# DeltaNet's values and two branches' gated outputs transposed by VectorE and a DRAM round trip

## The chip, the cores and the metric

One Trainium2 chip, one of its cores. The metric is device time in microseconds for one execution of the whole program; the profile is of one such execution. The engines are TensorE (PE, matmuls, with its weight loads as PEld), VectorE (DVE), ScalarE (ACT), GpSimd (POOL) and SyncE (SP); POOL and SP are also the queues from which most transfers are issued.

## The reference

One decoder layer on 256 positions of width 2048, in f32. The parts that bear on the change:

```
h = rms_norm(x, attn_norm)
(c_q, c_kv, k_rope, gla_q, gla_k, gla_v, gla_g_lr, gla_r,
 gdn_qkv, gdn_b, gdn_a, gdn_z, merge) = split(h @ w_in)
y_mla = mla_branch(...)                      # latent attention
y_gla = gla_branch(...)                      # gated linear attention, 4 heads of 128 x 256
y_gdn = gdn_branch(...)                      # gated DeltaNet, 8 value heads of 128
mixed = sum of sigmoid(merge_i) * (y_i @ w_branch_i)
x = x + mixed @ w_out
x = x + conv_ffn(rms_norm(x, ffn_norm))
out = rms_norm(x, final_norm)

# gdn_branch: q, k, v = split(silu(causal_dwconv(gdn_qkv))); chunked delta rule gives o
return rms_norm(o, out_norm).reshape(B, S, GDN_W) * silu(z)
# gla_branch: chunked scan gives o
return rms_norm(o, out_norm).reshape(B, S, GLA_W) * silu(r)
```

## The kernel before

**Weights and products.** The run is a sequence of products of an activation (256 positions) with weights of 1024 to 5632 rows. SP brings the weights in pieces `raw` of 512 KB (four buffers). ACT rounds a piece to `hi` (L191), DVE takes the rest `lo` (L103); both have four buffers, so a piece can be split only when PE is done with the piece four before it. PE forms each product from three matmuls (hi with hi, hi with lo, lo with hi). `f_chunk` (L196 to L198) gives 512 columns with features on the partitions: eight pieces of 24 matmuls, in two PSUM banks. `t_chunk` (L247 to L249) gives 512 columns with positions on the partitions: eight pieces of 12 wider matmuls, in two banks. Accumulators come from four banks `acc`; small products and transposes use four banks `mix` (`ps` in the rows).

**Order.** The program is written in one order and a tile scheduler sets each engine's order from it: it issues what is ready by its own model of times and waits, and the chip then runs each engine's list as it stands. SBUF tiles come from pools by tag, each tag with a number of buffers. A pool of one stage (`r2`: tags M, hq, g, Pm, vt, t, w) is closed and the next (`r3`: lqkv, glr, gates, E, aT, t) opened over the same memory; a tile of the next waits for the tiles that lay where it lies.

**DeltaNet.** Values come out of a convolution as `gv` (features on partitions). The solver needs them with positions on partitions: L780 transposes them on PE, four to a group of two heads, and DVE multiplies by `vs` out of PSUM into `vt`. Four groups are worked in two pairs. The results `og` (positions on partitions) are scaled by `z` and `fg` on DVE, and `gated_out` turns them back: four transposes on PE (L864) per group, then `gained` makes `hi_y` (ACT, L300) and `lo_y` (DVE, L106) out of PSUM. The region then changes to `r3`, and the GLA query, key and value chunks follow: `lq` and `lk` (tag lqkv) are emptied from `acc` by DVE, `lv` by ACT and DVE. `gated_out` serves GLA too, on `ol` with the gates `rs`, after the merge of branch 2 and ahead of the merge of branch 1; its results are `hi_E` and `lo_E`.

**Turning by DVE.** The kernel already has another way: `turned` (L303) transposes blocks of 32 by 32 on DVE into `tr`, POOL writes `tr` to DRAM (`d_t`, L313), and POOL reads it back with the blocks in their places (`rd`, L319, four transfers to a group); `gained_sb` (L323) then does what `gained` does, out of SBUF. It is used for the merge's first three column blocks and for the first three of the second half's input.

Of the kernel before, what the change touches and what calls it, by code (L numbers as in the profile page):

```python
# [9 lines left out]
F32 = mybir.dt.float32  # L10
# [6 lines left out]
P = 128  # L17
# [38 lines left out]
def trunk(ctx, tc, A, out, dbg=None, stop=None):  # L56
    nc = tc.nc
    pe, dve, act, pool, sync = nc.tensor, nc.vector, nc.scalar, nc.gpsimd, nc.sync
    serial = [0]

    def nm(s):
        serial[0] += 1
        return f"{s}{serial[0]}"
# [3 lines left out]
    dp = ctx.enter_context(tc.tile_pool(name="scratch", bufs=1, space=bass.MemoryType.DRAM))  # L67
# [14 lines left out]
    def S(tag, shape=(P, 512), dt=F32, n=None):  # L82
        p, bufs = pools[tag]
        return p.tile(list(shape), dt, name=nm(n or tag), tag=tag, bufs=bufs)

    def PS(n="ps"):
        return pp.tile([P, 512], F32, name=nm(n), tag="mix")
# [7 lines left out]
    def keep(shape, n, dt=F32):  # L95
        return cp.tile(list(shape), dt, name=n)
# [5 lines left out]
    def tt(o, a, b, op, eng=None):  # L102
        (eng or dve).tensor_tensor(o, a, b, op=op)  # L103
# [4 lines left out]
    MUL, ADD, SUB = ALU.mult, ALU.add, ALU.subtract  # L108
# [184 lines left out]
    def gained(psb, gains, store):  # L293

        hi, lo = store.new()
        if not isinstance(store, Joint):
            hi, lo = ([v[:, j] for j in range(2)] for v in (hi, lo))
        for j, g in enumerate(gains):
            src = psb[:, j * 256:(j + 1) * 256]
            act.activation(hi[j], src, AF.Copy, scale=g)  # L300
            stt(lo[j], src, g, hi[j], MUL, SUB)

    def turned(src, tags, n=512):  # L303

        nk = n // P
        d = dp.tile([2 * P, n], F32, name=nm("d_t"))
        for t in range(2):
            v = S(tags[0], (P, n), n="tr")  # L310
            dve.transpose(v.rearrange("p (b k i) -> p k b i", b=4, k=nk),
                          src[t].rearrange("p (k b i) -> p k b i", b=4, k=nk))
            pool.dma_start(d[t * P:(t + 1) * P], v)  # L313
        dv = d.rearrange("(a j) (b k i) -> b j a k i", j=32, b=4, k=nk)
        res = []
        for g in range(nk // 2):
            r = S(tags[1], (P, 8, 2, 32), n="rd")
            for b in range(4):
                pool.dma_start(r[b * 32:(b + 1) * 32], dv[b, :, :, 2 * g:2 * g + 2])  # L319
            res.append(r)  # L320
        return res

    def gained_sb(r, gains, store):  # L323

        hi, lo = store.new()
        if not isinstance(store, Joint):
            hi, lo = ([v[:, j] for j in range(2)] for v in (hi, lo))
        for j, g in enumerate(gains):
            h_, l_ = (v[j].rearrange("p (a i) -> p a i", i=32) for v in (hi, lo))
            act.activation(h_, r[:, :, j], AF.Copy, scale=g)  # L330
            stt(l_, r[:, :, j], g, h_, MUL, SUB)
# [302 lines left out]
        stt(gdec[:, t, :], xg[:, t, :], -1.0, ea, MUL, MUL)  # L634


    sel = keep([P, 68], "sel", F32R)
    pool.memset(sel.bitcast(F32), 0.0)
    pool.memset(sel[:, 3:4].bitcast(F32), 1.0)
# [133 lines left out]
    for gp in ((0, 1), (2, 3)):  # L773

        vts = {}
        for g in gp:
            psb = PS().rearrange("p (t x) -> p t x", t=2)
            for a in range(2):
                for t in range(2):
                    pe.transpose(psb[:, t, a * P:(a + 1) * P], gvv[2 * g + a][:, t * P:(t + 1) * P], ident)  # L780
            vts[g] = S("vt", (P, 2, 2, P))
            tt(vts[g].rearrange("p t a d -> p t (a d)"), psb, vs[:, :, g:g + 1].to_broadcast([P, 2, 256]), MUL)
        for s in (32, 64):
            work = []
            Pms = {g: S("Pm", (P, 4, s), n="Pm") for g in gp}
            for p in range(64 // s):
                for g in gp:
                    b1, b2 = slice(2 * p * s, 2 * p * s + s), slice(2 * p * s + s, 2 * p * s + 2 * s)
                    psb = PS()
                    pv = [psb[:, k * 128:k * 128 + 4 * s].rearrange("p (u j) -> p u j", u=4) for k in  # L790
                          ((0, 1, 2) if s == 32 else (0, 2))]
                    work.append((b1, b2, pv, Pms[g], Ms[g], Ys[g], Xs[g]))
            for b1, b2, pv, Pm, M, Y, X in work:
                for u in range(4):
                    pe.matmul(pv[0][b2, u, :], M[b1, u, b2], X[b1, u, b1], start=True, stop=True, **sk)
                dve.tensor_copy(Pm[b2], pv[0][b2])
            for b1, b2, pv, Pm, M, Y, X in work:
                for u in range(4):
                    pe.matmul(pv[1][b1, u, :], Pm[b2, u, :], Y[b2, u, b2], start=True, stop=True, **sk)
                dve.tensor_scalar(Y[b1, :, b2], pv[1][b1], -1.0, None, op0=MUL)  # L800
            if s == 32:
                for b1, b2, pv, Pm, M, Y, X in work:
                    for u in range(4):
                        pe.matmul(pv[2][b2, u, :], Y[b2, u, b2], Pm[b2, u, :], start=True, stop=True, **sk)
                    dve.tensor_scalar(X[b2, :, b1], pv[2][b2], -1.0, None, op0=MUL)
        u0s, W0s, R1s, W1s = {}, {}, {}, {}
        for g in gp:
            u0s[g] = PS()
            for a in range(2):
                pe.matmul(u0s[g][:, a * P:(a + 1) * P], Ys[g][:, a * 2, :], vts[g][:, 0, a, :], start=True, stop=True)  # L810
            W0s[g] = S("w", (P, 2, P), n="W0")
            tt(W0s[g], u0s[g][:, :256].rearrange("p (a d) -> p a d", a=2), b3(wj[:, 0, 2 * g:2 * g + 2], P), MUL)
        for g in gp:
            for a in range(2):
                pe.matmul(u0s[g][:, 256 + a * P:256 + (a + 1) * P], hqs[g][1][:, 1, a, :], W0s[g][:, a, :],
                          start=True, stop=True)
            R1s[g] = S("w", (P, 2, P), n="R1")
            tt(R1s[g], vts[g][:, 1], u0s[g][:, 256:].rearrange("p (a d) -> p a d", a=2), SUB)
        for g in gp:
            u1 = PS()  # L820
            for a in range(2):
                pe.matmul(u1[:, a * P:(a + 1) * P], Ys[g][:, a * 2 + 1, :], R1s[g][:, a, :], start=True, stop=True)
            W1s[g] = S("w", (P, 2, P), n="W1")
            tt(W1s[g], u1[:, :256].rearrange("p (a d) -> p a d", a=2), b3(wj[:, 1, 2 * g:2 * g + 2], P), MUL)
        for g in gp:
            op = PS().rearrange("p (t a d) -> p t a d", t=2, a=2)
            q0, q1 = hqs[g]
            for a in range(2):
                pe.matmul(op[:, 0, a, :], q0[:, 0, a, :], W0s[g][:, a, :], start=True, stop=True)
                pe.matmul(op[:, 1, a, :], q0[:, 1, a, :], W0s[g][:, a, :], start=True, stop=False)  # L830
                pe.matmul(op[:, 1, a, :], q1[:, 0, a, :], W1s[g][:, a, :], start=False, stop=True)
            os_ = S("d", (P, 2, 2, P), n="og")
            dve.tensor_copy(os_, op)
            o_gdn.append(os_)
            for a in range(2):
                for t in range(2):
                    junk = S("t", (P, P), n="junk")
                    c = t * 8 + 2 * g + a
                    act.activation(junk, os_[:, t, a, :], AF.Square, accum_out=gst[:, c:c + 1])
# [12 lines left out]
    for t in range(2):  # L852
        dve.tensor_scalar(fg[:, t, :], fg[:, t, :], rx[:, t:t + 1], None, op0=MUL)

    def gated_out(o_tiles, f_of, zs, gcol, name, ytag):

        y = Act(8, ytag)
        for g in range(4):
            o = o_tiles[g]
            f_of(g, o, [zs[t][g // 2][:, (g % 2) * 256:(g % 2) * 256 + 256] for t in range(2)])  # L860
            psb = PS()
            for a in range(2):
                for t in range(2):
                    pe.transpose(psb[:, a * 256 + t * P:a * 256 + (t + 1) * P], o[:, t, a, :], ident)  # L864
            gained(psb, [half_gain[:, gcol + 2 * g + a:gcol + 2 * g + a + 1] for a in range(2)], y)
            if dbg is not None and ("y_" + name) in dbg:
                full = S("t", (P, 2, 256), n="dbg")
                tt(full, y.hi[g].bitcast(F32), y.lo[g], ADD)
                sync.dma_start(dbg["y_" + name][:, 2 * g:2 * g + 2, :], full)
        return y  # L870
# [51 lines left out]
            tt(ov, ov, z[t], MUL)  # L922
        tt(o, o, fg[:, :, 2 * g:2 * g + 2].unsqueeze(3).to_broadcast([P, 2, 2, P]), MUL)

    y_gdn = gated_out(o_gdn, scale_gdn, zs, 8, "gdn", "y")
    if stop == "gdn":
        return

# [137 lines left out]
            ov = o[:, t].rearrange("p a d -> p (a d)")  # L1066
            stt(ov, ov, fl8[:, 2 * g + t:2 * g + t + 1], z[t], MUL, MUL)

    y_gla = gated_out(o_gla, scale_gla, sr, 0, "gla", "E")
    if stop == "gla":  # L1070
        return

# [206 lines left out]
```

## Time and profile before

| | |
|---|---|
| median of 3 runs | 1680.28 us (1678.97 to 1680.73) |
| profiled execution | 1680.61 us, span 1678.8 us |
| PE busy | 1664.4 us, 99% of the span |
| PE weight loads | 1426.9 us, 85% |
| DVE busy | 1099.7 us, 66% |
| ACT busy | 820.1 us, 49% |
| POOL busy | 123.9 us, 7% |
| moved by DMA | 315.01 MB, mean 188 GB/s |

The page gives busy times over the whole span and the chain of work that ended last; groups of instructions have the line, the engine, the operation and the tiles (output, then inputs, buffer numbers left out), and the idle time ahead of them with what ended it. Transfers are shown with their time from issue to landing. Many rows carry the line of a helper, such as L103 for each two-operand operation of DVE, so tiles tell more than lines.

### The profile page before, as it was taken

Reading aid. Unit: us, or ns where it says so; the run is one execution under the profiler, and the core shown is the slowest. Engines: PE = TensorE matmul, PEld = TensorE weight load, DVE = VectorE, ACT = ScalarE, POOL = GpSimd, SP = SyncE. Lnnn points to the kernel's source line nnn. Section 1 sums busy time; section 2 is a strip of 40 time slices with the busy share of each in tenths; the row PEclk is TensorE's granted clock in tenths of the full one; section 3 lists DMA queues with packets and bytes.
Section 4 is the critical chain, followed back from the end, with each engine's and each line's share of the span. In section 5 each row is a group of like instructions: output and inputs, shape, how many; then the busy total and the mean of one; then the engine's idle time right before and its main releaser. Section 6 shows DMA issues by size and latency. Waiting matters only on the chain.

```text
span 1678.8 us, 24640 instructions
## 1 busy us (share of the span) xinstructions
PE 1664.4 (99%) x9468; PEld 1426.9 (85%) x9468; DVE 1099.7 (66%) x1721; ACT 820.1 (49%) x1132; POOL 123.9 (7%) x193
## 2 busy tenths in 40 slices
PE   9999999999999999999999999999999999999997
PEld 7999988878998888888888888888888888888886
DVE  6956788855745696665556766664566665456666
ACT  6554563433434655444545555554355553345454
POOL 1000013110000000002112100000000000000000
PEclk9999999999999999999999999999999999999999
DMA  7654456654466565558777665555665566665663
GB/s 255 166 187 130 145 170 181 203 161 152 146 187 198 163 197 157 181 189 255 240 220 243 216 190 187 188 187 191 193 194 188 189 189 195 193 190 189 194 186 119
DMA packets 168774, 315.01 MB, mean 188 GB/s; under 512 B 17786, under 2 KB 20530, under 8 KB 168656
## 3 DMA queue, kind: packets, MB, share of 16 engines
q1 hardware_dynamic: 163200, 301.83, 57.1%
q0 software_dynamic: 5424, 11.60, 2.4%
q8 instruction: 74, 1.21, 0.3%
q14 instruction: 44, 0.36, 0.1%
q10 hardware_dynamic: 32, 0.01, 0.0%
HBM read 307.63 MB, written 5.77 MB: 187 GB/s over the span
## 4 chain that ended last, share of the span: by engine, by line
PE 98%; DMA 1%; SPq 0%; ACT 0%; DVE 0%; issue 0%; ACTq 0%
PE acc L249 17%; PE acc L248 17%; PE acc L247 17%; PE acc L228 10%; PE mix L228 10%; PE acc L229 5%; PE mix L229 5%; PE acc L198 3%; PE acc L196 3%; PE acc L197 3%; DMA x<-in_x_dram 1%; PE ps L542 0%; PE acc L1203 0%; PE acc L1205 0%; PE acc L1204 0%; PE ps L541 0%
## 5 line engine op out<-in xcount | busy, mean ns | idle before, releaser
L103 DVE TENSOR_TENSOR lo<-raw,hi 128x1024 fp32r<-128x1024 f32 (+2 forms) x571 | 686.1, 1203 | 511.3 <-ACT hi L191 508.0
L191 ACT CAST hi<-raw 128x1024 fp32r<-128x1024 f32 (+2 forms) x555 | 582.3, 1049 | 725.1 <-PE acc L249 414.9
L248 PE MATMUL acc<-lo,hi_h 128*128 128x512 f32 x640 | 249.5, 392 | 0.0
L247 PE MATMUL acc<-hi,hi_h 128*128 128x512 f32 x640 | 247.3, 391 | 1.6 <-ACT hi_h L300 1.2
L249 PE MATMUL acc<-hi,lo_h 128*128 128x512 f32 x640 | 248.9, 391 | 0.0
L228 PE MATMUL acc<-hl_h,hi 128*128 128x512 f32 x704 | 246.3, 396 | 0.0
L228 PE MATMUL mix<-hl_h,hi 128*128 128x512 f32 x704 | 246.3, 395 | 0.0
L229 PE MATMUL mix<-hl_h,lo 128*128 128x256 f32 x704 | 196.0, 278 | 0.0
L229 PE MATMUL acc<-hl_h,lo 128*128 128x256 f32 x704 | 195.7, 279 | 0.0
L228 PEld LDWEIGHTS mix<-hl_h,hi 128*128 128x128 f32 x704 | 132.1, 188 | 31.5
L228 PEld LDWEIGHTS acc<-hl_h,hi 128*128 128x128 f32 x704 | 131.8, 188 | 30.9
L247 PEld LDWEIGHTS acc<-hi,hi_h 128*128 128x128 f32 x640 | 119.9, 188 | 27.6 <-ACT hi_h L300 1.6
L248 PEld LDWEIGHTS acc<-lo,hi_h 128*128 128x128 f32 x640 | 120.2, 188 | 24.9 <-DVE lo L103 0.5
L249 PEld LDWEIGHTS acc<-hi,lo_h 128*128 128x128 f32 x640 | 120.0, 188 | 24.3
L229 PEld LDWEIGHTS acc<-hl_h,lo 128*128 128x128 f32 x704 | 132.5, 188 | 0.6
L229 PEld LDWEIGHTS mix<-hl_h,lo 128*128 128x128 f32 x704 | 132.5, 188 | 0.0
L248 PE MATMUL acc<-lo,hi_f 128*128 128x512 f32 x320 | 124.3, 389 | 0.0
L247 PE MATMUL acc<-hi,hi_f 128*128 128x512 f32 x320 | 124.2, 389 | 0.0
L249 PE MATMUL acc<-hi,lo_f 128*128 128x512 f32 x320 | 124.0, 389 | 0.0
L198 PE MATMUL acc<-hi_h,lo 128*128 128x256 f32 (+1 forms) x400 | 114.1, 285 | 0.0
L196 PE MATMUL acc<-hi_h,hi 128*128 128x256 f32 (+1 forms) x400 | 114.1, 285 | 0.0
L197 PE MATMUL acc<-lo_h,hi 128*128 128x256 f32 (+1 forms) x400 | 113.9, 285 | 0.0
(399 smaller groups left out, 2265.9 us busy)
## 6 DMA issues: line engine op xcount, KB each, us to landing
raw<-in_w_in_dram SPq DMA_DIRECT2D x207, 512.0 KB, 3.4
raw<-in_ffn_w_up_dram SPq DMA_DIRECT2D x176, 512.0 KB, 4.3
raw<-in_ffn_w_down_dram SPq DMA_DIRECT2D x88, 512.0 KB, 4.7
raw<-in_w_out_dram SPq DMA_DIRECT2D x32, 512.0 KB, 4.7
raw<-in_w_branch_mla_dram SPq DMA_DIRECT2D x16, 512.0 KB, 3.8
raw<-in_w_branch_gdn_dram SPq DMA_DIRECT2D x16, 512.0 KB, 3.6
raw<-in_w_branch_gla_dram SPq DMA_DIRECT2D x16, 512.0 KB, 6.1
raw<-in_mla_w_ukv_dram SPq DMA_DIRECT2D x8, 512.0 KB, 4.0
```

The costliest lines, as they stand in the source:

```text
L103: (eng or dve).tensor_tensor(o, a, b, op=op)
L191: act.copy(hi[:, ks], raw[:, ks])
L196: pe.matmul(o, s_hi, m_hi, start=first, stop=False, skip_group_check=True)
L197: pe.matmul(o, s_hi, m_lo, start=False, stop=False, skip_group_check=True)
L198: pe.matmul(o, s_lo, m_hi, start=False, stop=last, skip_group_check=True)
L228: pe.matmul(banks[f], hi[:, kt, fs], joint[k], start=k == 0, stop=False, skip_group_check=True)
L229: pe.matmul(banks[f][:, :T], lo[:, kt, fs], joint[k][:, :T], start=False, stop=k == nk - 1, skip_group_check=True)
L247: pe.matmul(o, ah, hi[:, kt, :], start=first, stop=False)
L248: pe.matmul(o, ah, lo[:, kt, :], start=False, stop=False)
L249: pe.matmul(o, al, hi[:, kt, :], start=False, stop=last)
```

## The change

Three places that transposed on PE go the other way.

- Values: after L634 DVE turns each `gv` group in blocks of 32 into a `tr` tile (tag t) and POOL writes it to DRAM (`d_v`). Where L780 stood, POOL reads a group back in four transfers into `rd` (tag t), and DVE multiplies by `vs` in two instructions per group.
- `gated_out` of DeltaNet: `turned` with 256 columns (two transposes, two writes and four reads for a group) with the tags t and g, then `gained_sb`.
- `gated_out` of GLA: the same, both tags lqkv.

So 48 transposes leave PE (16 for values, 16 for each output). DVE gets 4 transposes of 128x512 and 16 of 128x256; POOL's queue gets 20 writes and 48 reads. The other lines of the kernel are as they were; the scheduler orders everything anew.

```diff
+    d_v = []
+    for g in range(4):
+        v = S("t", (P, 4, 4, 32), n="tr")
+        dve.transpose(v.rearrange("p b k i -> p k b i"), gv[g].rearrange("p a (t b i) -> p (a t) b i", t=2, b=4))
+        d = dp.tile([P, 4, 4, 32], F32, name=nm("d_v"))
+        pool.dma_start(d, v)
+        d_v.append(d.rearrange("(a j) b k i -> b j a k i", j=32))
...
         for g in gp:
-            psb = PS().rearrange("p (t x) -> p t x", t=2)
-            for a in range(2):
-                for t in range(2):
-                    pe.transpose(psb[:, t, a * P:(a + 1) * P], gvv[2 * g + a][:, t * P:(t + 1) * P], ident)
+            r = S("t", (P, 4, 2, 2, 32), n="rd")
+            for b in range(4):
+                pool.dma_start(r[b * 32:(b + 1) * 32].rearrange("p c a t i -> p c (a t) i"), d_v[g][b])
             vts[g] = S("vt", (P, 2, 2, P))
-            tt(vts[g].rearrange("p t a d -> p t (a d)"), psb, vs[:, :, g:g + 1].to_broadcast([P, 2, 256]), MUL)
+            for t in range(2):
+                dve.tensor_scalar(vts[g][:, t].rearrange("p a (c i) -> p a c i", i=32),
+                                  r[:, :, :, t].rearrange("p c a i -> p a c i"), vs[:, t, g:g + 1], None, op0=MUL)
...
-    def gated_out(o_tiles, f_of, zs, gcol, name, ytag):
+    def gated_out(o_tiles, f_of, zs, gcol, name, ytag, tags):
...
-            psb = PS()
-            for a in range(2):
-                for t in range(2):
-                    pe.transpose(psb[:, a * 256 + t * P:a * 256 + (t + 1) * P], o[:, t, a, :], ident)
-            gained(psb, [half_gain[:, gcol + 2 * g + a:gcol + 2 * g + a + 1] for a in range(2)], y)
+            r, = turned([o[:, t].rearrange("p a d -> p (a d)") for t in range(2)], tags, 256)
+            gained_sb(r, [half_gain[:, gcol + 2 * g + a:gcol + 2 * g + a + 1] for a in range(2)], y)
...
-    y_gdn = gated_out(o_gdn, scale_gdn, zs, 8, "gdn", "y")
+    y_gdn = gated_out(o_gdn, scale_gdn, zs, 8, "gdn", "y", ("t", "g"))
...
-    y_gla = gated_out(o_gla, scale_gla, sr, 0, "gla", "E")
+    y_gla = gated_out(o_gla, scale_gla, sr, 0, "gla", "E", ("lqkv", "lqkv"))
```

The order on the engines at the end of the DeltaNet branch. First place, DVE, before: `og_3339` is the last scaled output, `lo_4942` to `lo_5002` are weight pieces of the GLA key chunk, `lq` is the query chunk's result out of `acc`.

```order
L103 TENSOR_TENSOR og_3339<-og_3339,fg 128x512
L103 TENSOR_TENSOR lo_4942<-raw_4939,hi_4941 128x1024
L103 TENSOR_TENSOR lo_4972<-raw_4969,hi_4971 128x1024
L106 SCALAR_TENSOR_TENSOR lo_y_4608<-ps_4602,half_gain,hi_y_4607 128x256
L106 SCALAR_TENSOR_TENSOR lq_4659<-acc_4663,rbc 128x512
L106 SCALAR_TENSOR_TENSOR lo_y_4622<-ps_4616,half_gain,hi_y_4621 128x256
L106 SCALAR_TENSOR_TENSOR lo_y_4636<-ps_4630,half_gain,hi_y_4635 128x256
L106 SCALAR_TENSOR_TENSOR lo_y_4650<-ps_4644,half_gain,hi_y_4649 128x256
L106 SCALAR_TENSOR_TENSOR lo_y_4608<-ps_4602,half_gain,hi_y_4607 128x256
L106 SCALAR_TENSOR_TENSOR lq_4660<-acc_4664,rbc 128x512
```

DVE there in the changed kernel: `lo_5170` is the last piece of the key chunk, `lo_5204` to `lo_5258` are the first four of the value chunk, `tr_4689` is the last of the eight transposes.

```order
L103 TENSOR_TENSOR lo_5170<-raw_5167,hi_5169 128x1024
L311 STREAM_TRANSPOSE tr_4689<-og_3359 128x2x4x32
L103 TENSOR_TENSOR lo_5204<-raw_5201,hi_5203 128x1024
L103 TENSOR_TENSOR lo_5222<-raw_5219,hi_5221 128x1024
L106 SCALAR_TENSOR_TENSOR lo_y_4635<-rd_4629,half_gain,hi_y_4634 128x256 x2
L103 TENSOR_TENSOR lo_5240<-raw_5237,hi_5239 128x1024
L103 TENSOR_TENSOR lo_5258<-raw_5255,hi_5257 128x1024
L106 SCALAR_TENSOR_TENSOR lo_y_4656<-rd_4650,half_gain,hi_y_4655 128x256 x2
L106 SCALAR_TENSOR_TENSOR lo_y_4677<-rd_4671,half_gain,hi_y_4676 128x256 x2
L106 SCALAR_TENSOR_TENSOR lo_y_4698<-rd_4692,half_gain,hi_y_4697 128x256 x2
L106 SCALAR_TENSOR_TENSOR lq_4707<-acc_4711,rbc 128x512
L106 SCALAR_TENSOR_TENSOR lq_4708<-acc_4712,rbc 128x512
```

The first `lq` stood behind the first `lo_y` and two pieces of the key chunk; it now stands behind all `lo_y` and four pieces of the value chunk.

Second place, PE, before: a group's transposes (`ps_4644`) inside the query chunk, whose banks are `acc_4663` and `acc_4664`, and the start of the key chunk (`acc_4907`).

```order
L197 MATMUL acc_4664<-lo_h_220,hi_4877 128x256
L864 MATMUL ps_4644<-ident,og_3339 128x128 x4
L198 MATMUL acc_4664<-hi_h_219,lo_4878 128x256
L196 MATMUL acc_4664<-hi_h_219,hi_4877 128x256
L197 MATMUL acc_4664<-lo_h_220,hi_4877 128x256
```

PE in the changed kernel at the end of the key chunk (`acc_4956`) and the start of the value chunk, whose bank `acc_5199` is the one that `acc_4711` had.

```order
L198 MATMUL acc_4956<-hi_h_219,lo_5170 128x256
L196 MATMUL acc_4956<-hi_h_219,hi_5169 128x256
L197 MATMUL acc_4956<-lo_h_220,hi_5169 128x256
L198 MATMUL acc_4956<-hi_h_219,lo_5170 128x256
L247 MATMUL acc_5199<-hi_5203,hi_h_142 128x512
L248 MATMUL acc_5199<-lo_5204,hi_h_142 128x512
```

The transposes are gone, and the value chunk follows the key chunk directly in both kernels; the bank that it opens with is now emptied by the `lq` of the first place.

Third place, POOL's queue from the solver's results to the GLA inputs, before:

```order
L764 MEMSET Y_3001 128x512
L767 DMA Y_3001<-d_y 32x4x32 x4
L764 MEMSET Y_3009 128x512
L767 DMA Y_3009<-d_y 32x4x32 x4
L951 DMA glr_5767<-in_onerow_dram 1x16x16
```

and in the changed kernel:

```order
L788 DMA rd_3209<-d_v_2668 32x4x128 x4
L313 DMA d_t_4622<-tr_4623 128x256
L313 DMA d_t_4622<-tr_4626 128x256
L313 DMA d_t_4643<-tr_4644 128x256
L313 DMA d_t_4643<-tr_4647 128x256
L313 DMA d_t_4664<-tr_4665 128x256
L319 DMA rd_4629<-d_t_4622 32x8x64 x4
L313 DMA d_t_4664<-tr_4668 128x256
L313 DMA d_t_4685<-tr_4686 128x256
L319 DMA rd_4650<-d_t_4643 32x8x64 x4
L313 DMA d_t_4685<-tr_4689 128x256
L319 DMA rd_4671<-d_t_4664 32x8x64 x4
```

Between the solver and the GLA inputs the queue now has the values' reads and the eight writes and sixteen reads of the four groups; the last four reads (`rd_4692`) follow the rows shown.

## The prediction

> **What bounds the kernel now.** I read the busy times of the page first, then the chain that ended last, then TensorE's (PE) busy time by stretches of the span, then what PE waited for.
>
> ```profile
> PE 1664.4 (99%) x9468; PEld 1426.9 (85%) x9468; DVE 1099.7 (66%) x1721; ACT 820.1 (49%) x1132; POOL 123.9 (7%) x193
> ...
> PE 98%; DMA 1%; SPq 0%; ACT 0%; DVE 0%; issue 0%; ACTq 0%
> ```
>
> ```profile
> 17.00:270.00 253.00, 253.00 (x1698) 229.25 (x1697) 195.49 (x400) 138.84 (x237) 17.84 (x21) 1.00 0.55 167
> 270.00:460.00 190.00, 190.00 (x1202) 162.01 (x1202) 131.20 (x232) 75.77 (x109) 20.37 (x40) 1.00 0.56 169
> 460.00:720.00 260.00, 260.00 (x1651) 218.36 (x1650) 171.31 (x331) 130.66 (x163) 6.00 (x19) 1.00 0.58 180
> 720.00:1640.00 920.00, 920.00 (x4711) 783.36 (x4711) 568.63 (x683) 448.12 (x567) 73.21 (x96) 1.00 0.63 201
> ```
>
> ```profile
> PE acc L247 <- ACT hi_h L300: 1.2, 1, 1.2
> PE acc L1203 <- ACT hi_f L276: 1.1, 1, 1.1
> PE warm L159 <- DVE ones L155: 1.1, 1, 1.1
> PE ps L371 <- DMA x<-in_x_dram: 0.6, 2, 0.4
> PE acc L247 <- ACT hi L191: 0.5, 1, 0.5
> ```
>
> In the second fence stand, for each stretch, its length and the busy time of PE, of its weight loads, DVE, ACT and POOL, then the granted clock and the share of the DMA engines. From 17 to 1640 us PE is busy without a gap, and all its waits of the run come to 4.5 us, at the two ends. So whatever work is taken off PE between 17 and 1640 us shortens the run by its length, and every microsecond in which PE is made to wait there lengthens it by one. The other engines matter only where they stop PE. Every place that the change touches lies between 230 and 730 us.
>
> **What is taken off PE.** 48 transposes: 16 at L780 (values), 16 at L864 on `og` and 16 at L864 on `ol`.
>
> ```profile
> L780 PE MATMUL ps<-ident,gv x16: 272/272/273, 273.4 to 397.3; 128*128 128x128 f32 x16
> ...
> L864 PE MATMUL ps<-ident,og x16: 270/272/276, 453.9 to 456.1; 128*128 128x128 f32 x16
> ...
> L864 PE MATMUL ps<-ident,ol x16: 270/272/273, 706.2 to 715.6; 128*128 128x128 f32 x16
> ```
>
> ```profile
> 454.01 0.44 PE ps L864 x4
> ...
> 714.46 1.42 PE ps L864 x13
> ```
>
> The 272 ns of one are latency; what counts is the pitch. In the chain, four take 0.44 us and thirteen 1.42, 0.11 each. 48 x 0.11 = 5.3 us, all inside the gapless part: **-5.3 us**.
>
> **What is added, and where it hides.** DVE gets 4 transposes of 128x512 and 16 of 128x256.
>
> ```profile
> L311 DVE STREAM_TRANSPOSE tr<-x x6: 669/686/704, 869.9 to 914.0; 128x512 f32<-128x512 f32 x6
> ...
> L106 DVE SCALAR_TENSOR_TENSOR lo_d<-rd,hi_d x12: 416/418/426, 768.4 to 838.8; 128x256 fp32r<-128x256 f32 x12
> ```
>
> That is 4 x 0.69 + 16 x 0.34 (half the size, half the time: an estimate) = 8.2 us; the four products out of PSUM become eight of half the size out of SBUF, and a `lo_y` goes from 0.48 us to the 0.42 of `lo_d`. DVE has 57 us free in the first stretch, 59 in the second and 89 in the third, so its total costs nothing; the order on DVE is what counts. POOL gets 20 writes and 48 reads:
>
> ```profile
> L319 POOL DMA_DIRECT2D rd<-d_t x48: 582/584/613, 760.3 to 924.9; - x48
> ...
> DMA to landing us min/median/max: 3.4/5.2/6.7
> ```
>
> ```profile
> L313 POOL DMA_DIRECT2D d_t<-tr x12: 547/553/580, 752.6 to 915.0; - x12
> ...
> DMA to landing us min/median/max: 2.4/3.7/6.0
> ```
>
> 20 x 0.55 + 48 x 0.58 = 39 us of issue on a queue that is 7% busy. The traffic is 3 MB written and 3 MB read beside 315 MB, with the DMA engines at 0.56 to 0.58: no price by itself. SP's queue, which brings the weights, is passed by none of it.
>
> **Where PE will wait: the end of the DeltaNet branch.** This is the term that decides. In the profile, DVE and ACT do this there:
>
> ```profile
> 450.33 2.50 DVE L103 TENSOR_TENSOR og<-og,fg 128x512 f32<-128x512 f32 x4
> 452.75 2.41 DVE L103 TENSOR_TENSOR lo<-raw,hi 128x1024 fp32r<-128x1024 f32 x2
> 455.08 0.48 DVE L106 SCALAR_TENSOR_TENSOR lo_y<-ps,half_gain,hi_y 128x256 fp32r<-128x256 f32 x1
> 455.47 0.68 DVE L106 SCALAR_TENSOR_TENSOR lq<-acc,rbc 128x512 f32<-128x512 f32 x1
> ```
>
> ```profile
> 447.09 1.05 ACT L191 CAST hi<-raw 128x1024 fp32r<-128x1024 f32 x1 [1.83 <-PE acc L197]
> 449.97 1.05 ACT L191 CAST hi<-raw 128x1024 fp32r<-128x1024 f32 x1 [1.83 <-PE acc L197]
> ```
>
> `lq` empties the PSUM bank of the GLA query chunk within a fraction of a microsecond of the first `lo_y`, while PE is already in the key chunk. In the changed order (first place shown above) `lq` and `lk` stand behind all eight `lo_y` on DVE, because their SBUF tiles lie where the branch's `tr` and `rd` tiles lie, and those are read until the last `lo_y`. There are four accumulator banks: two hold the query chunk, two the key chunk, and the first matmul of the value chunk (second place) needs the first one back. So PE ends the key chunk and has nothing else in its order until `lq` is through. Behind the waiting `lo_y` on DVE stand the splits of the value chunk's weights and both `lk`.
>
> How long? Call E the end of the key chunk. A weight piece takes PE 2.88 us here (449.97 - 447.09) and four pieces are held.
> - By DVE: `lo_5258`, four rows ahead of `lq`, belongs to the piece that takes the slot of the key chunk's last piece, so its cast can begin only at E: 1.05 us of cast, 1.2 of `lo`, six `lo_y` of 0.42 and an `lq` of 0.68 make 5.5 us, with a tenth or two for the releases 5.7.
> - By POOL (third place): the last `tr` comes behind `lo_5170`, whose slot is free at E - 11.5, so at about E - 8.9. In the built program each transfer of this queue also waits for the one eight places ahead of it. With 0.58 us an issue, 3.7 us for a write and 5.2 for a read, the second group's reads go out from E - 9.3, the last write at E - 6.5, the third group's from E - 5.9, the last read of the fourth at E - 1.3, held up by the third before it. It lands at E + 3.9; cast, two `lo_y`, `lq` and the releases make it 6.0 to 6.5.
>
> The later of the two holds: **+6.3 us**. The ends: with reads of 3.4 us DVE's way governs and it is 5.7; with reads of 6.7 the extra 1.5 us counts in each of three rounds, and it is about 10. I take the median, since the DMA share here (0.56) is below that of the stretch in which it was measured (0.63).
>
> On this wait the Trainium skill, page "DMA: Bandwidth & Descriptors", section "Anatomy of one DMA — SWDGE (gpsimd) path", gives about 2.0 us fixed and bytes over 436 GB/s, so 2.15 us for a 64 KB read. By that POOL's way would be over before DVE's, and the sum below would be lower by 0.6. The row says 5.2 us for these reads, and the row is used.
>
> **What the wait does to PE's clock.** PE has not been idle this long anywhere before its end.
>
> ```profile
> 1660.00:1670.00 10.00, 8.95 (x54) 7.79 (x52) 8.03 (x26) 5.34 (x16) 0.00 (x0) 1.00 0.30 102
> 1670.00:1673.50 3.50, 0.00 (x0) 0.00 (x0) 2.87 (x13) 1.26 (x3) 0.00 (x0) 1.00 0.03 11
> 1673.50:1674.00 0.50, 0.00 (x0) 0.00 (x0) 0.00 (x0) 0.08 (x1) 0.00 (x0) 0.93 0.80 311
> 1674.00:1674.50 0.50, 0.00 (x0) 0.00 (x0) 0.00 (x0) 0.00 (x0) 0.00 (x0) 0.50 1.09 418
> ```
>
> ```profile
> 437.19 0.22 PE ps L829 x2
> ```
>
> ```profile
> 1.06 3.78 PE L159 MATMUL warm<-ones 128*128 128x128 f32 x16 [1.06 <-DVE ones L155]
> ```
>
> PE's last matmul ends near 1669; the granted clock falls to 0.50 at about 1673.9, some 5 us later. And the sixteen first matmuls of the run, after idleness, took 0.24 us each where a pair of the same shape later takes 0.22: they ran at half speed for 3.8 us (the clock column reads 1.00 there, the durations say otherwise). So 3.8 us at half speed lose 1.9 us. A wait of 6.3 us is longer than the 5 at the end: **+1.9 us**, between 0 (no drop) and 2.5.
>
> The Trainium skill, page "TensorE: Matmul & The Clock Gate", section "Part 1: The HAM clock gate (the "warmup" mystery)", has the clock halved after an idle window of about 3.4 us that runs free of the kernel. By it a 6.3 us wait need not hold a whole window: in one run of seven it would not (0.5 of 3.4), and the sum would be 1.9 lower; the trace, with one drop after 5 us, does not contradict it.
>
> **The other places.** Values: `rd` for groups 2 and 3 lies in the `t` tag and can only be issued late; DVE may stand at the product for up to 1.7 us (the read's 5.2 less the 3.4 at best), but between there and the solver's products PE has chunk matmuls in its order. GLA: the round trip runs beside the gate chunk of the merge, 96 matmuls of 0.23 us, 22 us; four groups at the pace above take about 18 to 20 from the first `tr`, so it is covered with 2 to 4 us left. The front: the squares before L648 share the `t` tag with the four written values and wait for those writes; PE's reads of them now stand about 95 rows further down, behind chunk matmuls, and I leave 1 to 2 us of margin. These three: 0, with 0 to 3 in the range.
>
> **Sum**, against the profiled execution (1680.61 us; its span is 1678.8, with 1.8 around it): -5.3 + 6.3 + 1.9 = +2.9. The median of the runs is 1680.28, 0.33 below; from it 1683.2 us.
>
> **Rivals.**
> - Wait, but no drop of the clock: -5.3 + 5.7 to 6.3 = +0.4 to +1.0, 1681.0 us. For it: the only drop seen came after 5 us, so 5.7 is close. Against it: the start shows that idleness halves the speed.
> - The wait does not come, and the time falls by the 5.3 us: 1675.0 us, the other side. The place is the `lq` row; it decides in this way if DVE reaches `lq` before E, which needs `lo_5258` not to hang on the key chunk's last piece. For it: such round trips are hidden elsewhere (the merge's `turned` cost PE no wait in the list above). Against it: the order on DVE puts it behind a piece that can't be cast before E, whatever the transfers do.
> - More than one wait: on top of the forecast the front's writes take 6.0 us instead of 3.7 (2.3 more) and the values' reads stop the solver's products by 1.7: +6.9, 1687.2 us. For it: the margins are of the size of the spread of the landings. Against: chunk matmuls stand in between.
>
> **How the numbers follow.** About 0.2%, 3.4 us, is what a measurement of this kernel can tell from no change: 1676.9 to 1683.6. The forecast (wait and clock, 1682.6 with a wait of 5.7 us to 1685.6 with reads of 6.0) has 0.60; no drop of the clock 0.17; more than one wait 0.15; no wait 0.08. The forecast's case straddles the bound: half of it, 0.30, lies above, with the third rival 0.45 slower; 0.30 + 0.17 = 0.47 the same; 0.08 faster. The range leaves out the case without a wait and the upper third of the case with several: 1680.0 to 1688.0.
>
> **What would show it.** No L780 or L864 on PE. One gap of 5.7 to 7 us on PE at the first L247 of the value chunk, near 480 us, released by DVE's `lq`; a granted clock of 0.50 behind it for about 4 us; ahead of `lq` on DVE six `lo_y` without a stop, or with one that DMA `rd` ended (POOL's way). POOL busy by about 39 us more. I am wrong if that gap is under 5 us, if there is a second gap of over a microsecond at L648, L805 or the first matmul on `hi_E`, or if the clock holds through the gap.

## The result and the profile after

| | before | changed |
|---|---|---|
| median of 5 runs | 1680.28 us (1678.86 to 1680.73) | 1689.76 us (1688.76 to 1690.35) |
| ratio | | 1.0057 (95%: 1.0046 to 1.0068) |
| profiled execution, span | 1680.61, 1678.8 us | 1688.76, 1687.0 us |

The change makes the kernel 9.5 us slower; 2.9 were forecast, with a range up to 1688.0. The profiled execution is the quickest of the five, so the traces explain 8.2 us of span.

The page of the changed kernel, busy times and chain:

```profile
PE 1665.5 (99%) x9420; PEld 1425.0 (84%) x9420; DVE 1108.1 (66%) x1745; ACT 819.8 (49%) x1132; POOL 162.3 (10%) x261
...
PE 95%; issue 3%; DMA 1%; POOL 1%; ACT 0%; DVE 0%; SPq 0%; ACTq 0%; POOLq 0%
```

What PE waited for, in the changed kernel (the two longest):

```profile
PE acc L247 <- DVE lq L106: 8.0, 1, 8.0
PE acc L1210 <- ACT hi_f L276: 1.1, 1, 1.1
```

PE has 48 transposes less to do and is yet busy 1.1 us longer. Of waits one is new: the first matmul of the GLA value chunk for DVE's `lq`, 8.0 us, at the place that was named. The chain of the changed kernel around it (start, length, what):

```profile
472.61 4.49 DMA d_t<-tr
...
477.67 1.33 POOL rd L319 x3
...
479.39 4.38 DMA rd<-d_t
...
483.87 0.52 ACT hi_y L330
...
484.41 0.44 DVE lo_y L106
...
485.21 0.69 DVE lq L106
485.91 0.14 issue
486.05 0.77 PE acc L247
```

PE's last key matmul ends at 478.07. The last write of the round trip goes out at 472.61 and takes 4.5 us, the fourth group's reads wait for it, take 1.7 to issue and 4.4 to land, then cast, `lo_y` and `lq` follow: POOL's way, not DVE's, ends last. POOL's own row for these reads:

```profile
477.67 2.30 POOL L319 DMA_DIRECT2D rd<-d_t  x4 [2.08 <-DMA d_t<-tr]
```

Behind the wait the granted clock is down (stretches of 1 us of the changed kernel; the columns as in the prediction):

```profile
488.00:489.00 1.00, 1.00 (x4) 0.81 (x3) 0.00 (x0) 0.00 (x0) 0.00 (x0) 0.50 0.00 0
489.00:490.00 1.00, 1.00 (x4) 0.77 (x4) 0.00 (x0) 0.00 (x0) 0.00 (x0) 0.69 0.00 0
```

A clock of 0.69 over 489 to 490 means half speed up to 489.62; from 486.05 that is 3.6 us at half speed, 1.8 lost. So far: -4.1 (what the transposes proved to be worth in the traces, below) + 8.0 + 1.8 = +5.7. The other 2.5 us of the 8.2 are in no wait and not in the clock. They had to be found.

### The profile page after: what moved, and what is told of

Its sections match the earlier page's. It is cut to its first block, busy times and chain, and to the rows that moved or that the text cites. A ratio compares the mean times of both kernels' runs of the same rounds, so it can differ in the third digit from the quotient of the medians.

```text
span 1687.0 us, 24708 instructions
## 1 busy us (share of the span) xinstructions
PE 1665.5 (99%) x9420; PEld 1425.0 (84%) x9420; DVE 1108.1 (66%) x1745; ACT 819.8 (49%) x1132; POOL 162.3 (10%) x261
## 4 chain that ended last, share of the span: by engine, by line
PE 95%; issue 3%; DMA 1%; POOL 1%; ACT 0%; DVE 0%; SPq 0%; ACTq 0%; POOLq 0%
PE acc L248 17%; PE acc L247 17%; PE acc L249 17%; PE acc L228 10%; PE mix L228 10%; PE acc L229 5%; PE mix L229 5%; PE acc L198 3%; PE acc L196 3%; PE acc L197 3%; DMA rd<-d_t 1%; PE ps L542 0%; PE acc L1210 0%; PE acc L1212 0%; PE acc L1211 0%
```

## The experiments

All runs are compared with the kernel before, whose median was 1680.0 to 1680.2 beside each of them. Differences between two variants are differences of their medians, unless a trace is named.

**DeltaNet's output alone.** Values and GLA's output put back on PE:

```diff
-    y_gla = gated_out(o_gla, scale_gla, sr, 0, "gla", "E", ("lqkv", "lqkv"))
+    y_gla = gated_out(o_gla, scale_gla, sr, 0, "gla", "E", None)
```

(With `None`, `gated_out` transposes on PE; the lines for the values are those of the kernel before. The rest of the edit is left out here.)

> Only DeltaNet's gated output goes by DVE and DRAM; values and GLA's output stay on PE as before. Theory A (one wait: the first lq stands behind all eight lo_y, 8.0 us, and the clock at half speed behind it, 1.8 us): 16 transposes off PE give -1.7, so about +8, 1688 us, with one gap of 7 to 9 us on PE released by DVE's lq. Theory B (some 3 to 5 us of the loss are spread over the values and GLA, by more transfers and more switching between small and large matmuls): +3 to +5, 1683 to 1685.

1687.69 us, ratio 1.0051 (1.0036 to 1.0065): theory A's figure, reached in another way. The wait was 4.6 us only:

```profile
PE acc L247 <- DVE lq L106: 4.6, 1, 4.6
```

```profile
479.91 1.23 DVE L103 TENSOR_TENSOR lo<-raw,hi 128x1024 fp32r<-128x1024 f32 x1 [1.65 <-ACT hi L191]
481.05 1.67 DVE L106 SCALAR_TENSOR_TENSOR lo_y<-rd,half_gain,hi_y 128x256 fp32r<-128x256 f32 x4
482.63 1.28 DVE L106 SCALAR_TENSOR_TENSOR lq<-acc,rbc 128x512 f32<-128x512 f32 x2
```

DVE goes without a stop from the last piece through four `lo_y` to `lq`: this is DVE's way, the lower bound of the prediction, one pair of `lo_y` shorter in this order. With some 2.4 us of clock and 1.4 to 1.7 us of transposes the sum is +5.5, and the span is 8.0 over that of before: 2.5 us are again in no wait. The loss comes with this one part, though the medians don't add: 7.5 and the -2.6 of the other two (next) make +4.9, and the whole gives +9.5, with a wait that is 3.4 us longer in its order.

**Values and GLA's output, DeltaNet's on PE** (only its call goes back to PE):

> The values and GLA's output go by DVE and DRAM, DeltaNet's gated output stays on PE. Theory A: 32 transposes less and no wait, -3.5, 1676.8 us; lq on DVE ahead of the outputs' work, no PE wait over 1.2 us. Theory B (a spread loss outside DeltaNet's output): 1680 to 1683 us, not faster than before.

1677.55 us, ratio 0.9986 (0.9977 to 0.9995): faster, by 2.6 us of the 3.5. No wait on `lq`. Theory B, a loss spread over these two, is out.

**The values alone.**

> Only the values go by DVE and DRAM. 16 transposes less: -1.8. Theory F: the solver's small matmuls stand in more pieces (in the run with values and GLA the large matmuls between 360 and 440 us took 1.5 us more than before), so about -0.5, 1679.7. Without that: 1678.4.

1679.18 us, ratio 0.9996 (0.9987 to 1.0005): 0.9 us, between the two forecasts and not separable from no change. In the traces it is 0.5 us, as theory F has it: the large matmul that starts at 203.80 us in the kernel before, ahead of the change, starts 1.28 us sooner here, and the one at 468.90, behind the solver, 1.77 us sooner. The 16 transposes took 1.7 us in the kernel before, but between 230 and 462 us PE now goes from large to small matmuls 44 times instead of 37. By difference GLA's output is worth 1.7 us, all that its 16 transposes took.

**Other memory for DeltaNet's round trip.**

```diff
+    pools["th"] = (wp, 4)
-    y_gdn = gated_out(o_gdn, scale_gdn, zs, 8, "gdn", "y", ("t", "g"))
+    y_gdn = gated_out(o_gdn, scale_gdn, zs, 8, "gdn", "y", ("th", "th"))
```

> All of the change, but DeltaNet's tr and rd tiles lie in the stream pool (tag th, four buffers), over which lq and lk do not lie. Theory A (the overlay is the cause): lq goes early on DVE, the gap on PE is gone and the 48 transposes count: -5.3, 1675 us. Rival C (the round trip itself is too long, wherever it lies): a gap on PE of some us stays, later, at the first merge that reads y of DeltaNet, or with th shared at the gates; 1680 or more. Theory B: 1678 to 1681.

1675.48 us, ratio 0.9974 (0.9964 to 0.9985), span 1673.8: faster than both kernels. Its list of PE's waits has none on `lq`, and the longest is one that was there before:

```profile
PE acc L1211 <- ACT hi_f L276: 1.1, 1, 1.1
```

The work is the same as in the changed kernel; only where twelve tiles lie differs, and the order that follows from it. The round trip is no shorter here (its last reads start at 491.5 us), but nothing that PE needs stands behind it. This also gives the price of the transposes free of the rest: 4.7 us by the medians, 5.0 by the spans. Of these 5.0, 0.9 stand in the trace before the change can act: the same matmul starts at 203.80 us in the kernel before and at 202.87 here. PE's order is the same up to 220 us in the traces of all variants, and this matmul starts anywhere from 202.52 to 204.17 us in them: that is the spread of executions, and 4.1 are the change's own.

And it is the measure for the missing part. Here are the same four large matmuls, counted from the first of the run, in the changed kernel and with the other memory:

```profile
203.52 0.28 PE L196 MATMUL acc<-hi_h,hi 128*128 128x256 f32 x1
486.05 0.77 PE L247 MATMUL acc<-hi,hi_h 128*128 128x512 f32 x1 [7.98 <-DVE lq L106]
490.08 0.39 PE L248 MATMUL acc<-lo,hi_h 128*128 128x512 f32 x1
671.70 0.39 PE L247 MATMUL acc<-hi,hi_h 128*128 128x512 f32 x1
```

```profile
202.87 0.28 PE L196 MATMUL acc<-hi_h,hi 128*128 128x256 f32 x1
477.26 0.40 PE L247 MATMUL acc<-hi,hi_h 128*128 128x512 f32 x1
479.56 0.39 PE L248 MATMUL acc<-lo,hi_h 128*128 128x512 f32 x1
658.49 0.39 PE L247 MATMUL acc<-hi,hi_h 128*128 128x512 f32 x1
```

The changed kernel is behind by 0.65, 8.79, 10.52 and 13.21 us, and by 13.2 to the end. So of the 13.2 us between the two spans 0.65 is the start of the run, 8.1 the wait, 1.7 the clock, and 2.7 come between 490 and 672 us, where PE neither waits nor has a lower clock.

**Where the 2.7 us are.** In PE's timeline of these two kernels I took each matmul from its start to the next one's start, over the stretch with GLA's small matmuls (491 to 680 us in the changed kernel, 480 to 664 with the other memory). Large matmuls that stand clear of small ones take 0.227 us in both. Those next to small ones take 2.7 us over that in the changed kernel and 0.8 with the other memory, and the same 365 small rows take 12.3 us instead of 11.6. That is 2.6 of the 2.7 us. Between 470 and 720 us PE goes from large to small matmuls 22 times in the changed kernel, 12 times before, 10 times with the other memory (and 23 times with DeltaNet's output alone). One such place of the changed kernel, `E` being GLA's small tiles:

```profile
520.68 0.61 PE L247 MATMUL acc<-hi,hi_h 128*128 128x512 f32 x2
521.23 0.33 PE L1032 MATMUL ps<-E 128*32 128x32 f32 x16
521.49 0.50 PE L248 MATMUL acc<-lo,hi_h 128*128 128x512 f32 x1
521.82 0.39 PE L249 MATMUL acc<-hi,lo_h 128*128 128x512 f32 x1
```

From the first large matmul behind a run to the next one it is 0.33 us (521.49 to 521.82) instead of 0.23; the two ahead of it take 0.55 instead of 0.46. The same matmuls stood from 589 us on before, in longer runs; why the scheduler moved them is not shown. To price a place, 32 small matmuls were added to the fast version, once after each group of six of the value chunks and once in a single run ahead of them:

```diff
+    pe.matmul(probe[:32, :32], ones[:, :32], ones[:, :32], start=True, stop=True)   # in t_chunk, or 32 times
```

> As the 32 matmuls apart, now with weights of 32 columns as GLA's small matmuls have (the ones before loaded 128 columns, 0.11 us a row for the load alone, which hid the price of the change-over). Theory F (a change-over between large and small costs PE about 0.25 us): 32 x 0.25 to 0.3 = 8 to 10 us over 1675.5. Rival G (no such price): under 2 us.

> The same 32 in one run ahead of the value chunks. Both theories: 64 rows at 0.012 to 0.03 us, 0.8 to 2 us over 1675.5, and too short for the clock to fall.

Apart 1688.43 us (ratio 1.0050, 1.0037 to 1.0062), together 1678.34 (0.9991, 0.9982 to 1.0000). One run costs 2.9 us, 32 places 13.0: 10.1 us for 31 more places, **0.33 us each**. Both are above their forecasts (8 to 10, and 0.8 to 2): a row of the single run took 0.035 us (2.21 over 64), not 0.012 to 0.03. The trace of the first, one place, and of the second, the whole run:

```profile
484.28 0.40 PE L249 MATMUL acc<-hi,lo_h 128*128 128x512 f32 x1
484.60 0.25 PE L251 MATMUL probe<-ones 128*32 128x32 f32 x2
484.78 0.50 PE L247 MATMUL acc<-hi,hi_h 128*128 128x512 f32 x1
485.12 0.39 PE L248 MATMUL acc<-lo,hi_h 128*128 128x512 f32 x1
```

```profile
477.45 2.21 PE L951 MATMUL probe<-ones 128*32 128x32 f32 x64
```

Twelve places more than in the version with other memory at 0.33 would make 4.0 us; the starts above have 2.6, 0.22 a place. So a place costs time in both, but the probe's price is not GLA's price. No run put the pieces together again with the wait left in.

A first try of the same with weights of 128 columns misjudged it:

> The change with DeltaNet's tiles in the stream pool (1675.5), and 32 small matmuls added (128x32 of ones, result unused), one after each six large ones of the GLA value chunks. Theory F (each change between small and large matmuls costs PE 0.2 to 0.3 us, which makes the 3.4 us that the changed kernel loses beside the wait and the clock, with 22 pieces of GLA's small matmuls in place of 10): 32 places at 0.25 to 0.35 give 8 to 11 us, 1683.5 to 1686.5. Rival G (only the matmuls themselves count, the 3.4 us have another cause): under 2 us, 1677.

> The same 32 small matmuls in one run ahead of the GLA value chunks. Both theories: 64 rows at 0.01 to 0.03 us, 1 to 2 us, 1676.5 to 1677.5. Theory F: 7 to 9 us less than with them apart; rival G: the same as apart.

Apart 1684.32 us (1.0026, 1.0015 to 1.0036), together 1687.30 (1.0042, 1.0029 to 1.0055): the run of small ones is the dearer. At first its rows take 0.11 us each, the load of 128 columns; then the clock falls, although PE has no gap:

```profile
481.00:482.00 1.00, 1.00 (x8) 1.00 (x7) 0.34 (x1) 0.88 (x2) 0.00 (x0) 0.56 0.66 199
482.00:484.00 2.00, 2.00 (x11) 2.00 (x11) 0.90 (x3) 0.03 (x1) 0.00 (x0) 0.50 0.83 248
```

(Stretches of the kernel with them together.) So this pair says nothing on the change-over, and something on the clock (at the end).

**The gap filled.** Matmuls of ones on PE between the key and the value chunk, 56 and then 28:

```diff
+    fill = PS("fill")
+    for _ in range(56):    # 28
+        pe.matmul(fill[:, :P], ones, ones, start=True, stop=True)
```

> All of the change, with 56 matmuls of ones by ones (128x128, 0.11 us each, 6.2 us) added on PE between GLA's key and value chunks, where it waits; their result is not used. The wait for lq ends when it did. Theory A with the clock term: the clock stays at 1.00, so 1.8 us less than the changed kernel, about 1688. Rival D (the clock is not what costs, the time behind the gap is bound by something else): the same as the changed kernel, 1689.8. Rival E (the fill delays the rest): 1690 or more.

1690.46 us, ratio 1.0063 (1.0050 to 1.0076). I had the size wrong: a matmul in f32 makes two rows, so the 56 took 12.4 us and outlasted the wait.

```profile
478.07 12.66 PE L948 MATMUL fill<-ones 128*128 128x128 f32 x112
490.49 0.47 PE L247 MATMUL acc<-hi,hi_h 128*128 128x512 f32 x1
490.80 0.39 PE L248 MATMUL acc<-lo,hi_h 128*128 128x512 f32 x1
491.03 0.40 PE L249 MATMUL acc<-hi,lo_h 128*128 128x512 f32 x1
```

The median says nothing on rival D, but the rows do: after the fill the value chunk starts at full pace (0.23 us from 490.80 to 491.03), where in the changed kernel it ran at half clock for 3.6 us. PE starts it 4.4 us later here (490.49 against 486.05) and the span is 2.2 longer (1689.2 against 1687.0), so about 2 us came back: the clock's 1.8, and a little more for two places fewer at which small matmuls interrupt large ones (20 instead of 22).

> As the filled gap, with 28 added matmuls of 128x128: in the run with 56 the trace showed two rows a matmul, 112 x 0.11 = 12.4 us, longer than the gap; 28 should take 6.2 of the 6.6 to 8.0 us for which PE waits. Theory A with the clock term: clock 1.00 behind the gap, 1.8 us less than the changed kernel, 1687.5 to 1688.3. Rival D (the clock costs nothing there): 1689.8, as the changed kernel.

1688.78 us, ratio 1.0050 (1.0036 to 1.0064), but the five runs go from 1686.2 to 1692.4, too far apart to tell 1.8 us. In the profiled one the round trip was late: PE waited 3.7 us on top of the fill, and the clock fell in that wait. Inconclusive by time. Here are the stretches in which the clock fell, in the changed kernel, with DeltaNet's output alone and with this short fill:

```profile
482.00:483.00 1.00, 0.00 (x0) 0.00 (x0) 0.00 (x0) 0.00 (x0) 0.50 (x2) 0.90 0.92 295
481.00:482.00 1.00, 0.00 (x0) 0.00 (x0) 1.00 (x4) 0.48 (x2) 0.00 (x0) 0.69 0.43 164
487.00:488.00 1.00, 0.00 (x0) 0.00 (x0) 1.00 (x3) 0.07 (x1) 0.00 (x0) 0.64 0.00 0
```

A mean of 0.90, 0.69 and 0.64 (the third column from the end) puts the fall at 482.8, 481.4 and 487.3 us; PE's last matmul ahead of it ended at 478.07, 478.91 and 484.68.

**Writes by ACT.**

```diff
-            pool.dma_start(d[t * P:(t + 1) * P], v)
+            (act if tags == ("t", "g") else pool).dma_start(d[t * P:(t + 1) * P], v)
```

> All of the change, with DeltaNet's eight writes issued by ACT instead of POOL. Theory A in its parts (the last write stood 3.5 us in POOL's queue behind the reads of the second group, and the fourth group's reads waited for it): the write goes at once, POOL's way ends before DVE's, and PE waits what DVE's way asks for, about 5 us with four lo_y behind the last piece; some 3 us less than the changed kernel, 1686 to 1687. Rival H (the reads' own pace governs, eight at a time): the wait stays at 7 to 8 us, 1689.8.

1687.53 us, ratio 1.0043 (1.0030 to 1.0057), 2.2 us less by the medians, but the two intervals overlap. The wait was 7.9 us in the profiled run, the slowest of the five; the quicker four have no trace. In this trace the write's place in POOL's queue is not what holds the wait:

```profile
467.59 0.81 ACTq L313 DMA_DIRECT2D d_t<-tr  x2
```

```profile
476.86 2.30 POOL L319 DMA_DIRECT2D rd<-d_t  x4 [2.60 <-DMA d_t<-tr]
```

The last write now goes out at 468.0, 4.6 us sooner than in the changed kernel, and the reads that need it still start only at 476.9: the last two writes took 7.2 and 8.3 us. Sooner issued, later landed. Whether the sooner write would help in the quicker runs is open. The load shows in the stretches of the changed kernel, and in one of before at the same place (the last but one column is the share of the DMA engines):

```profile
465.00:470.00 5.00, 5.00 (x44) 5.00 (x44) 3.27 (x5) 1.70 (x2) 4.71 (x9) 1.00 1.01 333
470.00:475.00 5.00, 5.00 (x44) 5.00 (x43) 2.92 (x4) 2.25 (x4) 3.48 (x6) 1.00 0.97 309
475.00:480.00 5.00, 3.07 (x26) 2.86 (x24) 2.48 (x3) 3.02 (x5) 2.92 (x7) 1.00 0.93 279
```

```profile
465.00:470.00 5.00, 5.00 (x44) 5.00 (x44) 1.80 (x2) 2.06 (x2) 0.00 (x0) 1.00 0.55 167
```

While the round trips run, the DMA engines are nearly full. But they were nearly full as well around the transfers of the kernel before from which the prediction took its landings (the first of the merge's round trips):

```profile
757.00:762.00 5.00, 5.00 (x24) 4.13 (x22) 2.45 (x2) 1.87 (x2) 1.66 (x3) 1.00 0.95 333
762.00:767.00 5.00, 5.00 (x24) 4.14 (x23) 2.22 (x2) 2.11 (x2) 3.00 (x6) 1.00 0.97 276
```

In the changed kernel the eight writes landed in 2.0 to 5.2 us (median 4.3) and the sixteen reads in 4.4 to 5.7 (median 4.9); the rows of before have 2.4 to 6.0 and 3.4 to 6.7. None is above the old ranges, so slower landings at a higher load do not explain the longer wait by themselves.

## Why the prediction was wrong

- *What bounds the kernel, and what PE's time is worth*: PE bounds it, as said. That work taken off PE "shortens the run by its length" is not right: it leaves out that the same matmuls take longer in another order. The values' transposes took 1.7 us and brought 0.9 by the medians, 0.5 in the traces.
- *48 transposes, -5.3*: 4.7 by the medians of the version with other memory, 4.1 in its trace. From start to start the 48 took 4.7 us in the kernel before, 0.10 each and not 0.11.
- *The wait at `lq`*: right in place, cause and releaser, and shown by moving twelve tiles. Mis-sized: 8.0 us instead of 6.3. The term that was off is POOL's way. The last write went out at E - 5.5 instead of E - 6.5 and landed in 4.5 us where I took 3.7; the fourth group's reads waited for it and not for the third group's, so the last read went out at E + 1.3 instead of E - 1.3. It landed in 4.4 us where I took 5.2: 2.6 later less 0.8 is the difference of the waits, to a tenth. The argument with the share of the DMA engines (0.56 against 0.63) compared means of long stretches; around the transfers themselves the share was 0.95 to 0.97 before (757 to 767 us) and 0.93 to 1.01 in the changed kernel (465 to 480 us).
- *The clock, +1.9*: 1.8, with some luck: the half clock outlasted the wait by 3.6 us here, but by 4.7 with DeltaNet's output alone, where 2.4 us were lost. The clock fell 4.7 us after PE's last matmul in the changed kernel, 2.5 us after it with DeltaNet's output alone (wait 4.6 us) and 2.6 with the short fill (wait 3.7) (the three rows under the filled gap). The page "TensorE: Matmul & The Clock Gate" of the Trainium skill, section "Part 1: The HAM clock gate (the "warmup" mystery)", has the clock halved after an idle window of about 3.4 us that runs free of the kernel. The differing delays agree with a window that runs free; the falls after 2.5 and 2.6 us do not agree with a whole idle window of 3.4, and the measurement decides.
- *"These three: 0"*, the other places: this is the step that failed and that puts the time outside the range. No wait came there, as said (DVE stood 2.5 us at the values' product, where 1.7 were allowed for, and PE went on). But the sum counted waits only. GLA's small matmuls, moved from 589 us into the value and gate chunks from 499 us on and cut into more pieces, cost 2.7 us that no list of waits shows, and the sum put nothing for it and gave no reason (the 0 to 3 us that the range left for these places were for waits). With the other terms at their size in the traces (-4.1, +8.1, +1.7) the sum is +5.7, 1686.0 us and inside the range; with the 2.7 it is +8.4, 1688.7 us and outside.
- *Rivals*: the wait without the drop of the clock and the change without a wait did not come; the latter is what the version with other memory does, at the 1675 us worked out for it. More than one wait did not come either.

The profiled runs differ by 8.2 us: +8.4, less 0.3 that the changed kernel is ahead at 203 us (203.52 against 203.80). The medians differ by 9.5. The other 1.3 us are not explained: the changed kernel's trace is of the quickest of its five runs, and the slower four have none.

## What to carry to other kernels

When a tile of a new stage lies over a buffer that a round trip still reads, the whole round trip stands between PE and its next accumulator bank: before moving work to idle engines, look for what lies over its buffers, and give it memory that nobody waits for (here 14 us between two kernels of equal work). Price a round trip by its whole chain (what each issue stands behind, write, read), not by the median of one landing: no landing here was above the range of the earlier ones, and the last read still went out 2.6 us late. And on a PE that is never idle, count the places at which small matmuls interrupt large ones: they cost time that no wait shows. Before calling a residue found, compare the starts ahead of the change: 0.7 of the 13.2 us between two traces was there before it could act.

## What the runs showed of the hardware

- Where a short run of small matmuls (32 columns) stands among large ones, PE loses time on both sides of it: 0.33 us a place with two added rows (31 places more, 10.1 us), 0.22 a place for GLA's own runs (12 places more, 2.6 us).
- The clock can fall while PE is busy: in a run of matmuls of 128x32 with weights of 128 columns, PE and its weight loads both busy all the time by the profile, it went to 0.50 after 3.6 us (from 477.5 to 481.1), while 12.4 us of 128x128 matmuls, with the same loads, kept it at 1.00.
- In waits of 4.6 and 3.7 us the clock fell 2.5 and 2.6 us after PE's last matmul.
- In the run with writes by ACT the first two writes of 128 KB landed in 1.7 and 1.9 us and the last two in 7.2 and 8.3, while the share of the DMA engines went from 0.52 (460 to 465 us) to 1.01 and 1.06 (465 to 475 us).
